# An S5 mixer's input projection taken four row groups at a time, in four PSUM banks, with the pieces around it in a new sequence

## The chip, the cores and the metric

The kernel runs on one core of a Trainium2 chip. TensorE (PE) multiplies matrices, VectorE (DVE) and ScalarE (ACT) do elementwise work, GpSimd (POOL) and SyncE (SP) mostly issue transfers, and here GpSimd does some additions too. Each engine works its own queue in order. The metric is device time in microseconds (us) of one execution, lower is better.

## The reference, cut to what matters

The program is two transformer blocks on 256 tokens of width 1024, all in fp32. The first block puts 16 meta tokens ahead, normalises, projects to 5640 columns and feeds two mixers from them. The S5 mixer, which the change touches, is a diagonal complex recurrence per group of 16 channels (32 groups, 64 states each):

```python
def _s5_mixer(u, lam_re, lam_im, log_dt, b_re, b_im, c_re, c_im, d_skip):
    uf = u.astype(f32).reshape(bsz, length, S5_GROUPS, S5_GROUP)
    ...
    bu = jnp.einsum("gph,blgh->blgp", b_bar, uf.astype(jnp.complex64))
    a = jnp.broadcast_to(lam_bar, (1, length, S5_GROUPS, S5_STATE))
    _, state = lax.associative_scan(_linear_recurrence_combine, (a, bu), axis=1)
    y = jnp.real(jnp.einsum("ghp,blgp->blgh", c_mat, state))
    return y + d_skip * uf

for layer in range(DEPTH):          # first block
    p = h @ w_in[layer] + b_in[layer]
    u_s5, q, k, v, o_pre, i_pre, f_pre, g_s5, g_m = _split_columns(p)
    y_s5 = _s5_mixer(u_s5, ...)
    z = jax.nn.gelu(y_s5) @ s5_w_glu[layer]
    y_s5 = z[..., :D_MODEL] * jax.nn.sigmoid(z[..., D_MODEL:])
    hm = _mlstm_mixer(q_h, k_h, v_h, i_pre, f_pre)
    y_m = (jax.nn.sigmoid(o_pre) * _head_norm(hm, ...)) @ m_w_out[layer]
    mix = jax.nn.sigmoid(g_s5) * y_s5 + jax.nn.sigmoid(g_m) * y_m
    h = _layer_norm(ALPHA * h + mix @ w_o[layer], ...)
    # then the FFN
```

The second block (block attention, gated delta rule, a mixture of experts) follows and is not touched.

## The kernel before, in words

**The projection and its fillers.** `block1` projects in pieces of 256 columns (`in_proj`). A piece is two halves of 24 matmuls each (`ps_mm<-hTh,whi`, `hTl,whi`, `hTh,wlo`: the fp32 product from rounded high and low parts); each half fills one of the two `ps_mm` banks, and ScalarE empties it (`gth`). The weights of a piece come as `w`; ScalarE rounds them to `whi`, VectorE takes `wlo = w - whi`, and for a share of the pieces a GpSimd transfer forms `wlo` (L614). After each piece of v, og, gs and gm (four each, in this order) the S5 mixer is advanced by some pieces of its own, the mLSTM mixer by some of its own. `SCHED` is the list of S5 pieces per projection piece; what is left after gm runs behind the last projection piece (`step(s5, 100)`).

**The S5 mixer.** It works on four blocks c of 128 channels (eight groups of channels on 128 partitions, in four row groups r of 32 partitions). Its pieces are:

- `meta`: the 16 meta tokens.
- `elem(c, rr)`: for each row group of `rr` one `ps_acc` bank, the input projection (`ps_acc<-u,BT`, 32 rows of the array), and `turn`, which rotates the phases: two VectorE operations that read the bank (`s5z<-ps_acc,rot` and `s5t<-ps_acc,rot`) and two GpSimd additions (`s5z<-s5z,s5t`). `s5t` has two buffers.
- `chain(c)`: the recurrence, four times a carry (`s5c`, small `s5z` operations) and two scans over 256 elements (L821).
- `prod(c, rr)`: the rotation back, `s5q<-s5z,rot` and `s5z<-s5z,rot`, one of each for each row group.
- `cproj(c)`, which follows `prod(c, (2, 3))` in its piece: the output projection (`ps_acc<-s5q,CT` and `ps_acc<-s5z,CT`, 32 columns of the array each), then the skip term and GELU on `u`: VectorE `u<-u,FA,ps_acc`, ScalarE `gel_t`, VectorE `gel_t` twice, ScalarE `gel_w`, VectorE `u<-gel_w,u`.

PSUM holds two `ps_mm` banks and six `ps_acc` banks. A scheduler puts each engine's instructions in an order at build time, from the dependences and its own costs; `SCHED` and the sequence of pieces shape it.

**The other mixer.** For each of four heads the mLSTM mixer forms `mw` and `mwm` (ScalarE, then VectorE from `ps_acc`), multiplies them with the values (`ps_acc<-vt,mw` and `ps_acc<-vt,mwm`, 12 matmul instructions that are called a vt group here) and takes statistics (`bn_s`). After the fourth head a chain of 8-column VectorE operations, here the **rsqrt chain** (`mve`, `rs_y`, `rs_t`, `mc`, `mnb`), gives the scale; ScalarE then scales all heads (`qk<-qk,mnb,mc` x8), PE transposes them (`ps_acc<-ident,qk`) and VectorE gates them (`og`).

**The mix.** After the projection, the output matrices of both mixers are streamed through the same weight buffers; the first matmuls there are `ps_mm<-ymh,whi`.

Of the kernel before, what the change touches and what calls it, by code (L numbers as in the profile page):

```python
# [83 lines left out]
PP = [9]  # L84
L1A = [2, 2, 2, 2]
ORD = "abcdefmnopyz"
SCHED = [2, 2, 2, 2, 2, 2, 1, 1, 1, 1, 1, 1, 1, 1]


def dap(t, offset, *dims):  # L90
# [3 lines left out]
class K:  # L94
# [660 lines left out]
    def s5(self, pool):  # L755
# [3 lines left out]
        def bcast(v, *lead):  # L759
            shp = [128] + list(lead) + list(v.shape[1:])  # L760
            for _ in lead:
                v = v[:, None]
            return v.to_broadcast(shp)
# [3 lines left out]
        def turn(dst, src, cos, sin, tmp, eng):  # L767
            self.tt(dst, src, cos, OP.mult)
            self.tt(tmp, src, sin, OP.mult)
            self.tt(dst[:, 0], dst[:, 0], tmp[:, 1], OP.add, eng=eng)  # L770
            self.tt(dst[:, 1], dst[:, 1], tmp[:, 0], OP.subtract, eng=eng)
# [19 lines left out]
        def elem(c, rr):  # L791
            ps = {}
            if c not in Z:
                Z[c] = pool.tile([128, 4, 2, 4, 64], F32, name="s5z", bufs=2)
            for r in rr:
                ps[r] = self.ps("acc")
            for i in range(2):
                for r in rr:
                    rs = slice(32 * r, 32 * r + 32)
                    self.mm(ps[r][:, 256 * i:256 * i + 256], self.BT[i][rs, c, :], self.u[rs, c, 16:], True, True)  # L800
            for r in rr:
                z = Z[c][:, :, :, r, :].rearrange("p j i t -> p i j t")
                p = ps[r].rearrange("p (i j t) -> p i j t", i=2, j=4)
                t = pool.tile([128, 2, 4, 64], F32, name="s5t", tag="s5t", bufs=2)
                turn(z, p, *[bcast(self.rot[i][:, 4 * c + r], 2, 4) for i in range(2)], t, G)

        def chain(c):
            gs = slice(4 * c, 4 * c + 4)
            d = flat(self.decay[:, gs])
            last = tail[c]  # L810
            for j in range(4):
                z = Z[c][:, j]
                first = z[:, :, :, 0]
                t = pool.tile([128, 2, 2, 4], F32, name="s5c", bufs=2)
                for i in range(2):
                    self.tt(t[:, i], last, self.carry[:, j > 0, i, None, gs].to_broadcast([128, 2, 4]), OP.mult)
                self.tt(first, first, t[:, 0], OP.add)
                self.tt(first[:, 0], first[:, 0], t[:, 1, 1], OP.subtract)
                self.tt(first[:, 1], first[:, 1], t[:, 1, 0], OP.add)
                for i in range(2):  # L820
                    self.V.tensor_tensor_scan(flat(z[:, i]), d, flat(z[:, i]), 0.0, OP.mult, OP.add)  # L821
                last = z[:, :, :, 63]

        def prod(c, rr):
            if c not in Q:
                Q[c] = pool.tile([128, 4, 2, 4, 64], F32, name="s5q")
            for r in rr:
                z, q = (v[:, :, :, r, :].rearrange("p j i t -> p i j t") for v in (Z[c], Q[c]))
                for i, o in ((0, q), (1, z)):
                    self.tt(o, z, bcast(self.rot[i][:, 4 * c + r], 2, 4), OP.mult, eng=G if r in PP and i == 0 else None)  # L830

        def cproj(c):
            p = self.ps("acc")
            for n, (ct, i, z) in enumerate(((0, 0, 0), (1, 1, 1), (2, 0, 1), (2, 1, 0))):
                for r in range(4):
                    rs = slice(32 * r, 32 * r + 32)
                    self.mm(p[rs, :256], self.CT[ct][:, c, rs], (Q, Z)[i][c][:, :, z, r, :], n == 0, n == 3)
            ur = self.u[:, c, 16:]
            self.stt(ur, ur, self.FA[:, 92 + c:93 + c], p[:, :256], OP.mult, OP.add)
            if "ys5" in self.dbg:  # L840
                self.nc.gpsimd.dma_start(self.dbg["ys5"][c * 128:(c + 1) * 128, :], ur)
            t = self.cv.tile([128, 256], F32, name="gel_t", tag="cv_y", bufs=2)
            w = self.cv.tile([128, 256], F32, name="gel_w", tag="cv_t", bufs=2)
            self.act(t, ur, AF.Square)
            self.ts(t, t, 0.044715, OP.mult, 1.0, OP.add)
            self.tt(t, t, ur, OP.mult)
            self.act(w, t, AF.Tanh, scale=math.sqrt(2.0 / PI))
            self.stt(ur, w, 1.0, ur, OP.add, OP.mult)
# [1 line left out]
        meta()  # L850
        yield
        for c in range(5):
            if c < 4:
                elem(c, (0, 1))
                yield
            if c:
                prod(c - 1, (0, 1))
                yield
            if c < 4:
                elem(c, (2, 3))  # L860
                yield
            if c:
                prod(c - 1, (2, 3))
                cproj(c - 1)
                yield
            if c < 4:
                chain(c)
                yield
# [151 lines left out]
    def block1(self):  # L1020
# [38 lines left out]
        s5 = self.s5(work)  # L1059
        n5 = iter(list(SCHED) + [0] * 30)  # L1060
        mo = self.mlstm_out()
# [5 lines left out]
        for i in range(4):  # L1067
            self.in_proj(1536 + 256 * i, 0, lambda c0, j, p: self.evac_v(work, c0 - 12 + j, p),
                         lambda: step(s5, next(n5)))
        for i in range(4):  # L1070
            self.in_proj(2560 + 256 * i, 16, lambda c0, j, p: self.evac_gate(
                work, self.og, 2 * i + j, 0, p, self.halfg[:, 2 * i + j:2 * i + j + 1]),
                lambda: (step(ml, 2), step(s5, next(n5))))
        step(ml, 10)
        for k, dst in ((0, self.gs), (1, self.gm)):
            for i in range(4):
                self.in_proj(3592 + 1024 * k + 256 * i, 16, lambda c0, j, p: self.evac_gate(
                    work, dst, 2 * i + j, 8 + 8 * k, p, self.hc[:, k:k + 1]),
                    lambda: (step(mo, 1), step(s5, next(n5))))
# [1109 lines left out]
```

## Time and profile before

| | |
|---|---|
| time, three runs | 939.01, 930.54, 942.08 us (median 939.01) |
| profiled execution, device time | 939.74 us |
| its span, first to last instruction | 938.0 us |
| mean granted TensorE clock | 0.961 |
| PE busy | 885.8 us, 94% of the span |
| DVE, ACT, POOL busy | 572.8, 429.4, 62.9 us |
| stretch with the mixers | about 95 to 248 us |

The span is what the profiler sees between the first and the last instruction; the device time holds 1.7 us more. Busy shares are averages over the program: in the mixer stretch VectorE and GpSimd have a larger part of the work than afterwards. A granted clock of 1.00 is 2.4 GHz, 0.50 is 1.2 GHz.

### The profile page before, as it was taken

To read this page: it belongs to the slowest core of one execution; us is meant where nothing else is said; L and a number is where in the kernel's file an instruction comes from. 1 tells how busy PE (TensorE), PEld (TensorE's weight loads), DVE (VectorE), ACT (ScalarE), POOL (GpSimd) and SP (SyncE) were. 2 spreads that over 40 slices of the span, in tenths; PEclk is the share of its full clock that TensorE was granted. 3 is DMA by queue.
4 is the path that set the end of the run, shared out by engine and by line. 5 is a ranking of instruction groups with operands and counts; after the bars stand their busy time and mean duration, and the time that the engine had idled before them with its cause. 6 is when DMAs were issued, how large, how long until landed. Compare 5 with 4: busy or idle time off the path is not lost.

```text
span 938.0 us, 16064 instructions
## 1 busy us (share of the span) xinstructions
PE 885.8 (94%) x6204; PEld 670.7 (72%) x6204; DVE 572.8 (61%) x1457; ACT 429.4 (46%) x828; POOL 62.9 (7%) x91
## 2 busy tenths in 40 slices
PE   7998989998999999999998999999989999999993
PEld 6997857688999899998887998886654443444431
DVE  6688797757689667665578798666463222323213
ACT  4485444485766146564452366577442111222102
POOL 2012332122000000000000010000000000000000
PEclk7899897899999999999999999999999999999997
DMA  7887654478696356656773543334969999999971
GB/s 187 193 201 174 159 116 101 100 159 202 205 296 216 115 180 180 181 180 194 258 263 95 180 134 99 129 121 163 398 240 342 377 400 408 409 408 403 405 254 49
DMA packets 134708, 208.05 MB, mean 222 GB/s; under 512 B 13801, under 2 KB 99026, under 8 KB 134626
## 3 DMA queue, kind: packets, MB, share of 16 engines
q1 hardware_dynamic: 131458, 195.95, 62.4%
q0 software_dynamic: 2880, 10.49, 6.0%
q8 instruction: 51, 0.84, 0.4%
q10 hardware_dynamic: 288, 0.52, 0.2%
q14 instruction: 31, 0.25, 0.1%
HBM read 195.40 MB, written 1.05 MB: 209 GB/s over the span
## 4 chain that ended last, share of the span: by engine, by line
PE 74%; DVE 12%; ACT 6%; DMA 5%; issue 2%; POOL 0%; SPq 0%; ACTq 0%; POOLq 0%; DVEq 0%
PE ps_acc L133 43%; PE ps_mm L133 25%; PE ps_wo L133 3%; PE ps_acc L137 2%; DVE wlo L140 2%; DVE s5z L821 2%; ACT whi L155 2%; DMA wlo<-w 1%; DMA w<-in_w_in_dram 1%; DVE cv_y L149 1%; ACT mo_P L152 1%; DVE s5z L140 1%; DMA w<-in_w_up_dram 1%; DMA w<-in_m_w_out_dram 1%; DMA ln_g<-in_ln_g_dram 1%
## 5 line engine op out<-in xcount | busy, mean ns | idle before, releaser
L155 ACT ACTIVATE whi<-w 128x1024 fp32r<-128x1024 f32 x150 | 157.8, 1056 | 149.7 <-PE ps_mm L133 90.0
L140 DVE TENSOR_TENSOR wlo<-w,whi 128x1024 fp32r<-128x1024 f32 x130 | 160.0, 1232 | 85.2 <-ACT whi L155 84.6
L133 PE MATMUL ps_mm<-hph,whi 128*128 128x256 f32 x424 | 122.1, 288 | 0.0
L133 PE MATMUL ps_mm<-hph,wlo 128*128 128x256 f32 x424 | 120.8, 285 | 0.0
L133 PE MATMUL ps_mm<-hpl,whi 128*128 128x256 f32 x424 | 120.4, 284 | 0.0
L133 PE MATMUL ps_acc<-w,xg 128*64 128x512 f32 x512 | 117.8, 599 | 0.0
L133 PE MATMUL ps_mm<-hTh,whi 128*128 128x256 f32 (+1 forms) x360 | 108.2, 301 | 4.1 <-ACT gth L152 2.8
L133 PE MATMUL ps_mm<-hTh,wlo 128*128 128x256 f32 (+1 forms) x360 | 105.9, 294 | 2.7 <-DVE wlo L140 2.0
L133 PE MATMUL ps_mm<-hTl,whi 128*128 128x256 f32 (+1 forms) x360 | 105.8, 294 | 0.0
L133 PEld LDWEIGHTS ps_acc<-w,xg 128*64 128x64 f32 x512 | 35.6, 137 | 68.2 <-issue 64.1
L133 PEld LDWEIGHTS ps_mm<-hph,whi 128*128 128x128 f32 x424 | 79.9, 189 | 1.8 <-issue 1.8
L133 PEld LDWEIGHTS ps_mm<-hph,wlo 128*128 128x128 f32 x424 | 79.9, 188 | 1.2 <-issue 1.2
L133 PEld LDWEIGHTS ps_mm<-hpl,whi 128*128 128x128 f32 x424 | 79.9, 188 | 0.6 <-issue 0.6
L133 PEld LDWEIGHTS ps_mm<-hTh,whi 128*128 128x128 f32 x360 | 71.4, 199 | 9.5 <-ACT gth L152 3.1
L133 PEld LDWEIGHTS ps_mm<-hTh,wlo 128*128 128x128 f32 x360 | 71.3, 198 | 3.5 <-DVE wlo L140 2.2
L133 PEld LDWEIGHTS ps_mm<-hTl,whi 128*128 128x128 f32 x360 | 71.4, 198 | 1.2 <-issue 1.2
L152 ACT ACTIVATE mth<-ps_acc,cb 128x256 f32<-128x256 f32 x16 | 7.6, 475 | 119.8 <-PE ps_acc L133 119.8
L133 PE MATMUL ps_acc<-w,mhT 128*32 128x512 f32 x512 | 61.3, 594 | 1.0 <-DVE mhT L2011 1.0
L149 DVE SCALAR_TENSOR_TENSOR mth<-mth,ps_acc 128x256 f32<-128x256 f32 x16 | 6.7, 421 | 82.5 <-ACT mth L152 82.5
L140 DVE TENSOR_TENSOR hpl<-ps_acc,hph 128x512 fp32r<-128x512 f32 x40 | 26.1, 687 | 50.6 <-ACT hph L155 50.6
L155 ACT ACTIVATE hph<-ps_acc 128x512 fp32r<-128x512 f32 (+1 forms) x44 | 23.8, 576 | 64.0 <-PE ps_acc L133 61.5
L133 PEld LDWEIGHTS ps_acc<-w,mhT 128*32 128x32 f32 x512 | 20.1, 110 | 35.6 <-issue 30.5
(603 smaller groups left out, 1772.5 us busy)
## 6 DMA issues: line engine op xcount, KB each, us to landing
w<-in_w_down_dram SPq DMA_DIRECT2D x46, 1024.0 KB, 13.6
w<-in_w_gate_dram SPq DMA_DIRECT2D x60, 512.0 KB, 10.4
w<-in_w_up_dram SPq DMA_DIRECT2D x60, 512.0 KB, 7.2
w<-in_w_in_dram SPq DMA_DIRECT2D x41, 512.0 KB, 4.4
w<-in_w_in_dram SPq DMA_DIRECT2D x16, 1024.0 KB, 8.9
w<-in_w_up_dram SPq DMA_DIRECT2D x16, 1024.0 KB, 5.7
wlo<-w POOLq DMA_DIRECT2D x20, 512.0 KB, 5.1
w<-in_m_w_out_dram SPq DMA_DIRECT2D x4, 1024.0 KB
```

The source lines that it names most:

```text
L133: self.PE.matmul(out, lhsT, rhs, start=start, stop=stop, **kw)
L137: self.PE.transpose(out, in_, self.ident[:n, :n])
L140: (eng or self.V).tensor_tensor(out, a, b, op)
L149: (eng or self.V).scalar_tensor_tensor(out, a, s, b, op0, op1, **kw)
L152: self.S.activation(out, in_, func, bias=bias, scale=scale, **kw)
L155: self.S.activation(out, in_, AF.Copy)
L821: self.V.tensor_tensor_scan(flat(z[:, i]), d, flat(z[:, i]), 0.0, OP.mult, OP.add)
```

## The change

`elem` is called once for each block with all four row groups, so that its 16 matmul instructions write four `ps_acc` banks, and not twice with two. The piece that held its second half is gone, and the sequence for a block c is now: the first two products of block c-1, `elem(c)`, the other two products and the output projection of c-1, the chain of c. That makes 17 pieces of 21, and `SCHED` places them anew: 20 of its pieces ran inside the projection and one behind it before; now all 17 run by the last piece of gs, none in gm.

```diff
-SCHED = [2, 2, 2, 2, 2, 2, 1, 1, 1, 1, 1, 1, 1, 1]
+SCHED = [2, 2, 1, 2, 1, 2, 1, 2, 1, 1, 1, 1]
...
         for c in range(5):
-            if c < 4:
-                elem(c, (0, 1))
-                yield
             if c:
                 prod(c - 1, (0, 1))
                 yield
             if c < 4:
-                elem(c, (2, 3))
+                elem(c, (0, 1, 2, 3))
                 yield
             if c:
                 prod(c - 1, (2, 3))
                 cproj(c - 1)
                 yield
             if c < 4:
                 chain(c)
                 yield
```

| projection piece | S5 pieces before | S5 pieces after |
|---|---|---|
| v0 to v3 | meta, e0a; e0b, ch0; e1a, p0a; e1b, p0b | meta, e0; ch0, p0a; e1; p0b, ch1 |
| og0 to og3 | ch1, e2a; p1a, e2b; p1b; ch2 | p1a; e2, p1b; ch2; p2a, e3 |
| gs0 to gs3 | e3a; p2a; e3b; p2b | p2b; ch3; p3a; p3b |
| gm0 to gm3 | ch3; p3a; none; none | none |
| behind the projection | p3b | none |

(e is `elem`, ch `chain`, p `prod`; a is row groups 0 and 1, b is 2 and 3; `cproj(c)` is part of p b.)

The instructions are the same on every engine; their order differs from the first S5 piece to the start of the mix, and the SyncE queue is unchanged.

VectorE, between the chain and the products of block 0. Before:

```order
L140 TENSOR_TENSOR s5z_1458<-ps_acc_1459,rot0_556 128x2x4x64
L140 TENSOR_TENSOR s5t_1465<-ps_acc_1459,rot1_557 128x512
L140 TENSOR_TENSOR s5z_1458<-ps_acc_1460,rot0_556 128x2x4x64
L140 TENSOR_TENSOR s5t_1470<-ps_acc_1460,rot1_557 128x512
L140 TENSOR_TENSOR s5q_1475<-s5z_1237,rot0_556 128x2x4x64 x2
L140 TENSOR_TENSOR s5z_1237<-s5z_1237,rot1_557 128x2x4x64 x2
L140 TENSOR_TENSOR s5q_1475<-s5z_1237,rot0_556 128x2x4x64 x2
L140 TENSOR_TENSOR s5z_1237<-s5z_1237,rot1_557 128x2x4x64 x2
L140 TENSOR_TENSOR wlo_1765<-w_1761,whi_1764 128x1024
L140 TENSOR_TENSOR s5z_1458<-ps_acc_1558,rot0_556 128x2x4x64
```

After, from the second row of the products (`s5z_1237` is block 0 in both, its products are the rows that read it with `rot`; rows that read a `ps_acc` are the turns of block 1):

```order
L140 TENSOR_TENSOR s5z_1237<-s5z_1237,rot1_557 128x2x4x64 x2
L140 TENSOR_TENSOR s5q_1380<-s5z_1237,rot0_556 128x2x4x64
L140 TENSOR_TENSOR s5z_1463<-ps_acc_1464,rot0_556 128x2x4x64
L140 TENSOR_TENSOR s5t_1476<-ps_acc_1464,rot1_557 128x512
L140 TENSOR_TENSOR s5z_1463<-ps_acc_1465,rot0_556 128x2x4x64
L140 TENSOR_TENSOR s5t_1481<-ps_acc_1465,rot1_557 128x512
L140 TENSOR_TENSOR s5z_1463<-ps_acc_1466,rot0_556 128x2x4x64
L140 TENSOR_TENSOR s5t_1486<-ps_acc_1466,rot1_557 128x512
L140 TENSOR_TENSOR s5z_1463<-ps_acc_1467,rot0_556 128x2x4x64
L140 TENSOR_TENSOR s5t_1491<-ps_acc_1467,rot1_557 128x512
L140 TENSOR_TENSOR s5z_1237<-s5z_1237,rot1_557 128x2x4x64
L140 TENSOR_TENSOR s5q_1380<-s5z_1237,rot0_556 128x2x4x64
```

All four turns of block 1 now stand between the third and the last products of block 0; before, two stood ahead of all products and two behind them.

VectorE, at the rsqrt chain after the fourth head. Before:

```order
L149 SCALAR_TENSOR_TENSOR rs_y_2174<-rs_t_2175,rs_y_2174 128x8
L140 TENSOR_TENSOR rs_t_2175<-rs_y_2174 128x8
L149 SCALAR_TENSOR_TENSOR rs_t_2175<-rs_t_2175,mve_2168 128x8
L149 SCALAR_TENSOR_TENSOR rs_y_2174<-rs_t_2175,rs_y_2174 128x8
L140 TENSOR_TENSOR mc_2167<-mc_2167,rs_y_2174 128x8
L149 SCALAR_TENSOR_TENSOR mnb_2187<-mc_2167,mst_1671 128x8
L140 TENSOR_TENSOR s5z_2269<-ps_acc_2270,rot0_556 128x2x4x64
```

After, from the last turn of block 3 on (`s5z_2172` is block 3):

```order
L140 TENSOR_TENSOR s5z_2172<-ps_acc_2176,rot0_556 128x2x4x64
L140 TENSOR_TENSOR s5t_2200<-ps_acc_2176,rot1_557 128x512
L140 TENSOR_TENSOR rs_t_2213<-rs_y_2212 128x8
L140 TENSOR_TENSOR wlo_2444<-w_2440,whi_2443 128x1024
L149 SCALAR_TENSOR_TENSOR rs_t_2213<-rs_t_2213,mve_2206 128x8
L140 TENSOR_TENSOR s5z_2172<-s5z_2172,s5c_2408 128x8
L149 SCALAR_TENSOR_TENSOR rs_y_2212<-rs_t_2213,rs_y_2212 128x8
L140 TENSOR_TENSOR s5z_2172<-s5z_2172,s5c_2408 128x4 x2
L140 TENSOR_TENSOR rs_t_2213<-rs_y_2212 128x8
L821 SCALAR_TENSOR_TENSOR s5z_2172<-s5decay_558,s5z_2172 128x256
L149 SCALAR_TENSOR_TENSOR rs_t_2213<-rs_t_2213,mve_2206 128x8
L821 SCALAR_TENSOR_TENSOR s5z_2172<-s5decay_558,s5z_2172 128x256
```

The four turns of block 3 now stand inside the rsqrt chain, of which the excerpt has the last, and behind them a weight's `wlo`, the first carries and two scans of `chain(3)`; `mnb` follows five rows further down.

ScalarE, at the scaling of the heads. Before:

```order
L155 ACTIVATE whi<-w 128x1024
L152 ACTIVATE gth<-ps_mm,bh 128x256
L152 ACTIVATE wlo<-w 128x1024
L152 ACTIVATE qk<-qk,mnb,mc 128x256 x8
L152 ACTIVATE gs<-gth,hc 128x256
L152 ACTIVATE gth<-ps_mm,bh 128x256
L155 ACTIVATE whi<-w 128x1024
```

After (`gel_t` and `gel_w` belong to the GELU of block 2):

```order
L155 ACTIVATE whi<-w 128x1024
L152 ACTIVATE qk<-qk,mnb,mc 128x256 x8
L152 ACTIVATE gel_t<-u 128x256
L155 ACTIVATE whi<-w 128x1024
L152 ACTIVATE wlo<-w 128x1024
L152 ACTIVATE gel_w<-gel_t 128x256
L152 ACTIVATE gth<-ps_mm,bh 128x256
```

The next `gth` now stands behind the scaling and the GELU of block 2, with two weights' rounding between them.

## Rows read from the trace of the kernel before

**Rows 1.** From the page: busy time of the engines, and PE's busy tenths and granted clock in 40 equal slices of the span (23.45 us each).

```profile
PE 885.8 (94%) x6204; PEld 670.7 (72%) x6204; DVE 572.8 (61%) x1457; ACT 429.4 (46%) x828; POOL 62.9 (7%) x91
...
PEclk7899897899999999999999999999999999999997
```

**Rows 2.** Busy time of each engine in four stretches of the mixers (us busy, number of instructions, then granted clock, DMA share, GB/s).

```profile
119.20:130.00 10.80, 8.82 (x62) 5.13 (x61) 10.80 (x16) 2.25 (x5) 5.64 (x7) 0.84 0.66 147
130.00:153.00 23.00, 20.53 (x105) 15.85 (x103) 19.29 (x52) 10.20 (x22) 6.80 (x8) 0.78 0.48 115
153.00:182.00 29.00, 27.14 (x166) 18.82 (x166) 20.11 (x57) 12.95 (x31) 5.54 (x6) 0.88 0.49 110
...
222.60:248.00 25.40, 22.22 (x188) 20.61 (x187) 14.44 (x24) 18.07 (x30) 1.73 (x2) 0.93 0.83 225
```

**Rows 3.** PE's waits between 95 and 275 us: what waited for what, us in total, times, longest.

```profile
PE ps_acc L133 <- DVE mwm L149: 4.3, 2, 2.5
PE ps_mm L133 <- ACT gth L152: 2.8, 1, 2.8
PE ps_acc L133 <- DVE s5q L140: 2.0, 2, 1.7
PE ps_mm L133 <- DVE gm L140: 1.1, 1, 1.1
```

**Rows 4.** PE's timeline at two of the input projections (start, duration of the group, number of records; the next row's start ends it), and at one vt group with its successor.

```profile
95.06 2.08 PE L133 MATMUL ps_acc<-u,BT 32*128 32x256 f32 x8
...
104.04 1.13 PE L133 MATMUL ps_acc<-u,BT 32*128 32x256 f32 x8
105.11 0.39 PE L133 MATMUL ps_mm<-hTh,whi 128*128 128x272 f32 x1
...
159.46 1.13 PE L133 MATMUL ps_acc<-vt,mw 128*128 128x257 f32 x4
160.53 0.70 PE L133 MATMUL ps_acc<-u,BT 32*128 32x256 f32 x4
```

**Rows 5.** PE's timeline at the output projection of block 0 and the projection matmul behind it (in brackets the idle time before the row and who ended it).

```profile
121.45 0.62 PE L133 MATMUL ps_acc<-s5q,CT 128*32 128x256 f32 x2
...
124.66 1.24 PE L133 MATMUL ps_acc<-s5q,CT 128*32 128x256 f32 x3 [1.72 <-DVE s5q L140]
...
128.55 0.39 PE L133 MATMUL ps_mm<-hTh,whi 128*128 128x256 f32 x1
```

**Rows 6.** VectorE's timeline from the chain of block 0 to the products of block 0.

```profile
110.44 0.45 DVE L140 TENSOR_TENSOR s5z<-s5z,s5c 128x8 f32<-128x8 f32 x3 [1.32 <-POOL s5z L140]
...
117.82 0.67 DVE L140 TENSOR_TENSOR s5z<-ps_acc,rot 128x512 f32<-128x512 f32 x1
118.40 0.68 DVE L140 TENSOR_TENSOR s5t<-ps_acc,rot 128x512 f32<-128x512 f32 x1
...
120.19 2.08 DVE L140 TENSOR_TENSOR s5q<-s5z,rot 128x512 f32<-128x512 f32 x2
...
125.13 1.28 DVE L140 TENSOR_TENSOR s5z<-s5z,rot 128x512 f32<-128x512 f32 x2
126.33 1.21 DVE L140 TENSOR_TENSOR wlo<-w,whi 128x1024 fp32r<-128x1024 f32 x1
```

**Rows 7.** GpSimd's timeline: the additions of two row groups (four instructions), once beside turns and once beside products.

```profile
100.38 2.84 POOL L140 TENSOR_TENSOR s5z<-s5z,s5t 128x256 f32<-128x256 f32 x4 [13.55 <-DVE s5t L140]
...
119.17 3.68 POOL L140 TENSOR_TENSOR s5z<-s5z,s5t 128x256 f32<-128x256 f32 x4 [5.37 <-DVE s5t L140]
```

**Rows 8.** Windows of 2 us, as in rows 2: behind the stop at 124.66, and around a short stop before 266.

```profile
125.00:127.00 2.00, 2.00 (x17) 0.81 (x18) 2.00 (x4) 0.00 (x0) 0.00 (x0) 0.50 0.87 164
...
264.00:266.00 2.00, 1.19 (x11) 0.98 (x9) 1.46 (x2) 1.46 (x2) 0.00 (x0) 1.00 1.07 364
266.00:268.00 2.00, 1.75 (x15) 1.78 (x16) 1.79 (x3) 1.65 (x2) 0.00 (x0) 1.00 0.83 266
```

**Rows 9.** PE's timeline at the first, third and fourth vt group (the fourth's last row).

```profile
140.15 0.70 PE L133 MATMUL ps_acc<-vt,mwm 16*128 16x257 f32 x2 [2.47 <-DVE mwm L149]
...
171.31 0.70 PE L133 MATMUL ps_acc<-vt,mwm 16*128 16x257 f32 x2 [1.86 <-DVE mwm L149]
...
190.41 1.13 PE L133 MATMUL ps_acc<-vt,mw 128*128 128x257 f32 x4
```

**Rows 10.** The rsqrt chain and what hangs on it: VectorE's first and last row of it, ScalarE's scaling, PE's first transposition.

```profile
191.66 0.42 DVE L338 BATCH_NORM_STATS2 bn_s<-ps_acc 128x6 f32<-128x256 f32 x1
...
195.58 0.17 DVE L149 SCALAR_TENSOR_TENSOR mnb<-mc,mst 128x8 f32<-128x8 f32 x1
...
196.22 4.03 ACT L152 ACTIVATE qk<-qk,mnb,mc 128x256 f32<-128x256 f32 x8
...
196.86 0.33 PE L137 MATMUL ps_acc<-ident,qk 128*128 128x128 f32 x1
```

**Rows 11.** ScalarE at the GELU of block 2 and PE's next projection matmul.

```profile
221.58 0.42 ACT L152 ACTIVATE gel_t<-u 128x256 f32<-128x256 f32 x1 [3.92 <-DVE u L149]
224.08 0.42 ACT L152 ACTIVATE gel_w<-gel_t 128x256 f32<-128x256 f32 x1 [2.09 <-DVE gel_t L140]
...
225.86 0.39 PE L133 MATMUL ps_mm<-hTh,whi 128*128 128x256 f32 x1 [2.83 <-ACT gth L152]
```

**Rows 12.** PE at the end of the projection: the output projection of block 3 and the first matmul of the mix.

```profile
245.21 0.64 PE L133 MATMUL ps_acc<-s5q,CT 128*32 128x256 f32 x8
...
247.48 0.50 PE L133 MATMUL ps_mm<-ymh,whi 128*128 128x256 f32 x2 [0.34 <-ACT ymh L155]
```

## Prediction, on record before the result

> **What bounds the kernel now.** I read the page's busy times and its 40 slices first. PE is busy for 94% of the span [rows 1], so a change can win only what PE stands still, what it does at half clock, or work that it is spared; whatever it wins in the first block, the later stages carry to the end, since they are untouched and PE-bound too. The slices show a granted clock of 1.0 nearly everywhere but in the first quarter. So the next view is the stretches of the mixers: there PE has 0.78 to 0.93 of full clock, and in each of these stretches it is idle for some us [rows 2]. The waits name the causes [rows 3]: PE stands for `mwm`, for `gth`, for `s5q`, some 9 us in all. The half clock comes behind these stops: 0.50 in the 2 us behind the stop of 1.72 [rows 5, 8]. Its price is the stretch times what the clock lacks: 10.8 x 0.16 = 1.7, 23 x 0.22 = 5.1, 29 x 0.12 = 3.5 and 25.4 x 0.07 = 1.8 us [rows 2], 12.1 together, 3.0 for a stop on average. A stop of 0.81 us ahead of 266 has clock 1.00 on both sides [rows 8]. So what the kernel can gain here is about 9 + 12 us, and the question is not whether VectorE has time on average but at which moments PE arrives before it.
>
> **The input projection itself.** One piece of two row groups takes 1.06 us at full clock (104.04 to 105.11) and 2.0 at half clock [rows 4]. Its eight instructions last as long as four full-height ones of the vt group (1.07 us, 159.46 to 160.53) [rows 4], so two row groups do run side by side. No row shows four of them side by side. Bounds: 1.06 for all 16 instructions if they do (4.2 us of PE saved over the program), 2.12 if they don't (nothing saved). I take 1.06, since two groups lost nothing. For four row tiles the Trainium skill (TensorE: Matmul & The Clock Gate, Part 3: Packing small matmuls, measured speedup) gives 3.07x, not 4x; by that 16 instructions of 0.27 us would take an estimated 1.4 us, and the sum below would come out 0.7 us higher. The two side by side here (2.0x) neither bear that out nor contradict it.
>
> **Block 0: earlier start, longer stop.** At the start all four turns of block 0 follow each other. GpSimd needs 1.42 us for a row group beside turns (2.84 for two) [rows 7]; from 100.38 four of them end at about 106, and the chain starts there and not at 110.44, where it had waited 1.32 for GpSimd [rows 6]. From 106 VectorE has, in its new order: the chain 7.4 (110.44 to 117.82), a `wlo` 1.2, five products at 0.6, all eight turn operations of block 1 at 0.6 (117.82, 118.40) [rows 6]: about 122.4. Then the last products, with GpSimd's additions beside them: two took 2.08 there rather than 1.2 [rows 6]. The first of them end at 124.4, the last, behind another `wlo`, at 126.8. PE is there earlier, since two input projections before it are spared: 121.45 - 2.1 = 119.3 [rows 5]. It works off the last group at half clock in 2 us and leaves the output projection at about 129.0, 0.45 later than now (128.55). As the stop is some 7 us rather than 2, I add 0.75 of half clock: **1.2 us lost.** The four spared projections of this part are worth nothing, they become waiting. By the Trainium skill (SBUF — State Buffer, Who interferes with whom) a VectorE operation with two SBUF inputs and a GpSimd operation that reads SBUF exclude each other, and one that reads PSUM does not; the 3.68 us of additions beside products against 2.84 beside turns [rows 7] agree. Eight turns in a row are by that the good place for the additions, which is in the sum.
>
> **Heads one to four.** PE came to the first vt group at 137.68 and stood 2.47 [rows 9]. After, it comes 1.2 later and behind four more projection matmuls (0.12 each): 139.4. VectorE, from 126.8: chain 7.4, a `wlo` 1.2, the GELU's four operations 1.6, three products 1.8, `mw` and `mwm` 0.9, together 139.7. So the stop shrinks to 0.3, and the 5.1 us of half clock behind it go. The stop of 1.86 at the third group with its 3.5 goes likewise [rows 2, 9]. New ones come: a `ps_mm` bank waits for a `gth` that now stands behind block 0's or 1's `gel_w` (rows 11 show what such a place costs: up to 2.8), worked out at 1.2; and `mwm` of the third head stands behind turns, worked out at 1.05 (between 0 and the 2.5 of rows 9). Both are too short, I take it, to bring the half clock. With one input projection spared (1.06): -1.2 - 0.3 + 2.47 + 5.1 + 1.86 + 3.5 + 1.06 - 1.2 - 1.05 = **10.2 ahead** at the fourth vt group; with that of block 3, 11.3.
>
> **The rsqrt chain.** Here it is given back. Now `mnb` is done 4.2 us after the fourth vt group (191.55 to 195.75), ScalarE scales the heads (4.03 for eight) and PE's first transposition runs at 196.86 [rows 10], with no stop over 0.3. After, the eight turn operations of block 3 stand inside that chain (4.8 us), a `wlo` (1.2), a wait for GpSimd and the carries (1.0) and two scans (1.3): 4.2 + 8.3 = 12.5 us after the vt group, and the first scaled head at 13.0. PE has the input projection (1.06), 66 projection matmuls (7.9) and small gaps until it needs it: 9.4. It stops for 3.5 us, and the half clock follows. The next obstacle is close: the output projection of block 3 has one matmul in PE's queue ahead of the next projection piece, and its `s5q` stands on VectorE behind the rest of the chain (some 9 us behind `mnb`), 21.3 after the vt group. The `gth` for the next bank, behind the scaling, GELU and two weight roundings on ScalarE, comes at about the same time. PE without stops would be at 13.4. Loss 7.9, whichever part of it is stop and which half clock: 11.3 - 7.9 = **3.4 ahead.** Bounds: 3.5 (one stop and no half clock) to 11 (both stops and twice 3.0).
>
> **The last pieces and the mix.** The stop of 2.83 behind block 2's GELU [rows 11] goes with its 1.8 of half clock: that GELU is over by then, and block 3's stands with its VectorE steps next to each other. 8.0 ahead. The output projection of block 3 leaves the end of the projection (245.21 to 247.0) [rows 12]; in return nothing is won, since the weights of the mix come on a chain that starts from the last projection pieces and ends at the short stop before 266 [rows 8]: that stop grows from 0.8 to 2.5. 6.3 ahead at 266. All stops of 1.72 and longer in these rows were followed by half clock, so I take the cheapest of the four, 1.8, for this one: **4.5 ahead.** The weight transfers that GpSimd issues come behind up to eight additions rather than four; four additions take 2.8 to 3.7 us [rows 7], so a transfer that had no slack would cost PE that much; I take 0, since no row of PE's waits names such a transfer [rows 3].
>
> **Sum.** 939.74 - 4.5 = 935.2. The profiled execution lies 0.7 over the median of the runs (939.01), so 935 stands for both.
>
> **Rivals.**
> (1) *Slower: short stops also bring the half clock.* The forecast has stops of about 1.0 to 1.4 us at the `gth` of block 0's GELU, at the third `mwm` and at `s5q` of block 3 without one. No row has a stop between 0.81 (not followed) and 1.72 (followed) [rows 5, 8]. If the line lies at 1 us, three more half clocks of 3.0 make 944, slower than before. It decides from a stop of about 1 us.
> (2) *The rsqrt chain is not late.* If PE comes to the transposition later, or VectorE gets through the turns sooner (GpSimd's part in it is an estimate), the stop of 3.5 falls under 1 us and its half clock goes: 6 to 7 us better, 928. For it: the sum for VectorE is 12.5 with nothing overlapped. Against it: the order is fixed and all of its parts have rows.
> (3) *The pieces don't do what they say:* four row groups in four banks take 2.12 us. Block 2 and 3 then lose 1.06 each, block 0 starts its turns later by 2 at half clock and passes that on to the first stop, about half of it: 938. By the rows that two groups share the array at no loss I hold this unlikely.
>
> **How the numbers follow.** Forecast 0.45 (931 to 938), slower 0.25, rival 2 0.2, rival 3 0.1. The range reaches from 926, rival 2 with the mix's half clock gone too, to 944, rival 1. 2% are 18.8 us, about what a measurement of this kernel can tell from no change (its three runs lie 11.5 us apart); all stops, half clocks and spared projections together are some 25 us, so over 2% faster takes nearly all of them: 0.04. Over 2% slower needs new stops at more places than the order shows: 0.04. Within 2%: 0.92.
>
> **What the profile after would show.** PE's `u,BT` in four groups of 16 records, 1.1 us each at full clock (2.1: rival 3). A stop of 6 to 8 us for `s5q` or `s5z` at 119 to 127, and none over 0.5 at the first vt group. Clock 1.00 from about 132 to 165. A wait for ScalarE's `qk` at about 190 of 3 to 4 us, with the clock at 0.50 behind it, and one for `s5q` or `gth` at about 200. No stop over 1 us in the pieces of gm. I would be wrong if the clock falls around 160 to 170 (rival 1) or if PE is not stopped at `ident,qk` (rival 2).

## The result, and the profile after

The changed kernel takes 942.37 us (median of 20 runs, 937.40 to 945.97); the kernel before, beside it, 937.48 (20 runs). The ratio is 1.0052 (95% interval 1.0033 to 1.0072): **slower by half a percent**, less than the 2% of the verdict, but the interval lies above 1. The forecast was 935, faster by half a percent. A later measurement gave 942.11 (12 runs) and 1.0057 (1.0028 to 1.0087).

The profiled execution says the opposite: 937.79 us, 2 us less than that of before. So the profile alone can't explain the result, and one of the questions below is why. First what it shows, against [rows 1 to 3]: busy times, four of the stretches (and 182 to 205, which had no stop over 0.3 us before), and PE's waits in the mixers.

```profile
PE 877.2 (94%) x6204; PEld 664.6 (71%) x6204; DVE 573.4 (61%) x1457; ACT 430.2 (46%) x828; POOL 61.0 (7%) x91
...
PEclk7898989989999999999999999998999999999997
```

```profile
119.20:130.00 10.80, 5.95 (x41) 3.43 (x42) 9.26 (x23) 0.65 (x2) 4.63 (x6) 0.68 0.66 153
130.00:153.00 23.00, 22.91 (x156) 17.34 (x158) 15.87 (x43) 14.10 (x33) 1.72 (x2) 1.00 0.55 127
153.00:182.00 29.00, 27.20 (x187) 21.06 (x176) 25.78 (x73) 14.99 (x35) 8.36 (x10) 0.94 0.48 110
182.00:205.00 23.00, 16.50 (x127) 12.94 (x126) 22.35 (x60) 14.32 (x24) 8.27 (x10) 0.90 0.57 131
...
222.60:248.00 25.40, 22.92 (x188) 22.03 (x187) 10.36 (x20) 18.60 (x37) 1.72 (x2) 1.00 0.93 244
```

```profile
PE ps_acc L133 <- DVE s5q L140: 6.8, 2, 4.7
PE ps_acc L137 <- ACT qk L152: 4.5, 1, 4.5
PE ps_mm L133 <- ACT gth L152: 1.8, 1, 1.8
PE ps_mm L133 <- ACT ymh L155: 1.6, 1, 1.6
PE ps_acc L133 <- DVE s5z L140: 1.6, 1, 1.6
PE ps_mm L133 <- DMA wlo<-w: 0.6, 1, 0.6
```

The half clock between 130 and 153 and the waits for `mwm` are gone; instead PE is idle for 6.5 us between 182 and 205. The stops one by one, from PE's timeline, with the two ends of the rsqrt chain on VectorE (answering to [rows 4, 5, 9, 10]):

```profile
92.88 2.09 PE L133 MATMUL ps_acc<-u,BT 32*128 32x256 f32 x16
...
108.94 1.15 PE L133 MATMUL ps_acc<-u,BT 32*128 32x256 f32 x16
110.01 0.39 PE L133 MATMUL ps_mm<-hTh,whi 128*128 128x272 f32 x1
...
122.49 0.63 PE L133 MATMUL ps_acc<-s5q,CT 128*32 128x256 f32 x1 [4.73 <-DVE s5q L140]
125.13 0.61 PE L133 MATMUL ps_acc<-s5z,CT 128*32 128x256 f32 x1 [1.56 <-DVE s5z L140]
...
161.95 0.39 PE L133 MATMUL ps_mm<-hTh,whi 128*128 128x256 f32 x1 [1.80 <-ACT gth L152]
...
179.96 0.43 DVE L338 BATCH_NORM_STATS2 bn_s<-ps_acc 128x6 f32<-128x256 f32 x1 [0.84 <-PE ps_acc L133]
...
192.60 0.17 DVE L149 SCALAR_TENSOR_TENSOR mnb<-mc,mst 128x8 f32<-128x8 f32 x1
...
193.46 0.47 PE L137 MATMUL ps_acc<-ident,qk 128*128 128x128 f32 x1 [4.48 <-ACT qk L152]
202.23 0.59 PE L133 MATMUL ps_acc<-s5q,CT 128*32 128x256 f32 x2 [2.02 <-DVE s5q L140]
...
244.13 0.51 PE L133 MATMUL ps_mm<-ymh,whi 128*128 128x256 f32 x2 [1.57 <-ACT ymh L155]
```

### The profile page after: what moved, and what is told of

Same layout as the page of the kernel before. It is cut to its first block, busy times and chain, and to the rows that moved or that the text cites. A ratio compares the mean times of both kernels' runs of the same rounds, so it can differ in the third digit from the quotient of the medians.

```text
span 936.0 us, 16073 instructions
## 1 busy us (share of the span) xinstructions
PE 877.2 (94%) x6204; PEld 664.6 (71%) x6204; DVE 573.4 (61%) x1457; ACT 430.2 (46%) x828; POOL 61.0 (7%) x91
## 3 DMA queue, kind: packets, MB, share of 16 engines
HBM read 195.40 MB, written 1.05 MB: 210 GB/s over the span
## 4 chain that ended last, share of the span: by engine, by line
PE 70%; DVE 9%; ACT 5%; issue 1%; DMA 1%; POOL 1%; ACTq 0%; POOLq 0%; DVEq 0%
PE ps_acc L133 41%; PE ps_mm L133 24%; PE ps_wo L133 4%; PE ps_acc L137 2%; DVE wlo L140 2%; ACT whi L155 1%; DMA wlo<-w 1%; DVE cv_y L149 1%; ACT mo_P L152 1%; DVE s5z L821 1%; POOL s5z L140 1%; ACT h L155 1%; DVE r L149 0%; ACT g_FW L155 0%; DVE s5z L140 0%
## 5 line engine op out<-in xcount | busy, mean ns | idle before, releaser
L133 PEld LDWEIGHTS ps_acc<-w,xg 128*64 128x64 f32 x512 | 35.4, 137 | 67.8 <-issue 64.5
L133 PEld LDWEIGHTS ps_acc<-w,mhT 128*32 128x32 f32 x512 | 20.2, 110 | 35.6 <-issue 30.4
```

The source lines that it names most:

```text
L133: self.PE.matmul(out, lhsT, rhs, start=start, stop=stop, **kw)
```

## The experiments

Each execution lists its time and its mean granted clock. Time x (1 - clock) is what half clock took from PE in it, time x clock is the rest (full-clock work and idle time). This table has the averages over the timed runs and is used throughout. The mean clock is listed to three decimals, so the split of a single execution is good to half a us. Each kernel was compared with runs of the kernel before on the same chip; these are four sets in all, the clocks are from three of them. The sets are: changed; merge_only and rsqrt_first; changed again, late_block3 and merge_products_first; the other four. Between sets the ratios to before are the safer comparison, and the text gives both where they differ.

| kernel | runs | median us | ratio to before (95%) | half clock us | rest us |
|---|---|---|---|---|---|
| before (four sets) | 107 | 937.5, 939.4, 939.0, 938.1 | | 33.6 to 34.5 | 903.5 to 904.0 |
| changed | 20 | 942.4 | 1.0052 (1.0033 to 1.0072) | 35.2 | 906.7 |
| changed, again | 12 | 942.1 | 1.0057 (1.0028 to 1.0087) | 35.6 | 906.5 |
| merge_only | 12 | 936.1 | 0.9968 (0.9942 to 0.9994) | 34.0 | 901.3 |
| rsqrt_first | 12 | 940.1 | 1.0020 (0.9997 to 1.0044) | 33.8 | 905.7 |
| late_block3 | 12 | 933.9 | 0.9976 (0.9948 to 1.0003) | 33.7 | 900.2 |
| merge_products_first | 12 | 933.2 | 0.9959 (0.9927 to 0.9991) | 33.7 | 899.6 |
| sequence_only | 12 | 943.4 | 1.0062 (1.0032 to 1.0091) | 36.2 | 907.0 |
| bank_turned | 12 | 938.7 | 1.0020 (0.9993 to 1.0047) | 32.2 | 905.6 |
| merge_best | 12 | 932.1 | 0.9952 (0.9921 to 0.9983) | 32.5 | 899.6 |
| late_best | 12 | 930.7 | 0.9940 (0.9908 to 0.9971) | 30.2 | 900.4 |

**Both kernels again.** No edit.

> The kernel before once more, for a second profiled execution. Theory M (the change of the time is made in the mixers, between the first input projection of S5 and the first matmul of the FFN): that stretch took 218.8 us in the first profile (95.06 to 313.90); here it takes 214 to 217, since the first profile lies 2.3 us over the median. Theory O (the change is made outside, by where the half clock falls at the start and in the block attention): the stretch stays within 1 us of 218.8 and the rest moves.

> The kernel before, a third profiled execution. Theory M (the half clock behind one and the same stop differs from execution to execution): the stops of the mixers at the same places and lengths within 0.3 us, the half clock behind at least one of them of another length than in the first two. Rival (the half clock is fixed by the stop): the same stretches again, 3.4, 10.2, 6.8 and 3.4 us.

> The changed kernel once more, for a second profiled execution; its first one (937.8) is the second fastest of its 20 runs. Theory M: the mixer stretch, 216.6 us in the first profile (92.88 to 309.44), takes 219 to 224 here, with more half clock behind the stops at gth (1.8 us at 162), qk (4.5), s5q (2.1) and ymh (1.6). Theory O: the stretch stays within 1 us of 216.6 and the half clock behind the stop for mo_P near 640 or at the start makes the rest longer.

> The changed kernel once more, timed beside the others. Split of an execution's time into what the half clock takes (time x (1 - mean clock)) and the rest: in the first 20 runs of the change 35.2 and 906.7 us, in 23 of before 34.5 and 904.0. Theory M (more idle time in the mixers, 17 us for 10, less 4.2 us of spared projections, and the half clock not less than before over many executions): the rest again 2 to 3.5 us over before's, the half clock within 1.5 of it, 0.3 to 0.6% slower. Rival (the first measurement was of its chip): within 0.2% of before.

The profiled executions of before took 939.74, 939.62 and 941.20 us, those of the changed kernel 937.79, 939.71 and 936.96. The stretch from the first input projection to the FFN took 218.8, 219.3 and 219.2 before and 216.6, 217.1 and 216.2 after: theory M's stretches (214 to 217 before, 219 to 224 after) were not seen, and both stayed within 1 us of the first profiles, as theory O has it. The timed runs of the changed kernel came out as theory M of the last expectation has them: the rest 3.0 us over before's, half clock 1.2 over, 0.57% slower. All profiled executions of the changed kernel lie under its medians by 2.4 to 5.4 us, those of before over theirs by 0.2 to 2.3. By the split, profiled executions of before lose 36.6 to 38.5 us to half clock (timed 33.6 to 34.5), those of the change 30.0 to 34.8 (timed 35.2, 35.6), while the rest differs by 2.4 us in the profiled and by 2.5 to 3.2 in the timed ones. So it is the half clock on which profile and timing disagree, far more than the rest. Why the profiled executions fall where they do is open; three executions of each kernel are few, since half clock alone differs by 8 to 13 us between the timed executions of one kernel.

In the three profiles of before the half clock in the mixers stands in the same stretches, so the rival held there. For the changed kernel it did not. Here is PE in two of its executions, windows of 2 us at and behind the stop of 1.80 for `gth` (idle in the first row of each; PE's busy time comes first, the clock third from the right); first the first profile, then the third:

```profile
160.00:162.00 2.00, 0.20 (x2) 0.05 (x1) 1.42 (x6) 0.88 (x3) 0.55 (x1) 1.00 0.00 0
162.00:164.00 2.00, 2.00 (x12) 2.00 (x13) 1.97 (x9) 1.83 (x6) 0.00 (x0) 0.69 0.00 0
164.00:166.00 2.00, 2.00 (x12) 2.00 (x11) 1.93 (x8) 1.72 (x5) 0.00 (x0) 0.50 0.00 0
```

```profile
159.00:161.00 2.00, 0.20 (x2) 0.08 (x1) 1.45 (x6) 0.91 (x3) 0.52 (x1) 1.00 0.00 0
161.00:163.00 2.00, 2.00 (x17) 2.00 (x18) 1.97 (x9) 1.82 (x6) 0.00 (x0) 1.00 0.00 0
```

The same stop in the same kernel is followed by half clock once and not the other time. In the second profile it is followed by half clock too, so twice of three times.

**The merge without the new sequence.** Against the kernel before:

```diff
-                elem(c, (0, 1))
+                elem(c, (0, 1, 2, 3))
                 yield
...
             if c < 4:
-                elem(c, (2, 3))
                 yield
```

> The input projection of all four row groups in one piece, at the place of the first half of before, with the numbers and the sequence of before for all else (an empty piece where the second half was). Theory M with the sequence as cause: no turns inside the rsqrt chain beyond those of before's place for block 3, no stop at ident,qk over 1 us; 3 us faster to 2 slower than before. Rival (merging itself is the cause: all turns and additions of a block together hold VectorE up ahead of the products of the block before): a stop of 5 to 7 us at the output projection of block 0, and 3 to 6 us slower than before.

It is faster than before by 3 us, so the four banks are a gain. Theory M holds, at the edge of its range, and the rival is right about one thing: the stop at the output projection of block 0 is there (4.7 and 1.3 us), and yet the kernel is faster. The stop at `ident,qk` is 0.6 us.

**The sequence without the merge.** Against the changed kernel, `elem(c, (0, 1, 2, 3))` becomes `elem(c, (0, 1))` and `elem(c, (2, 3))` in one piece.

> The new sequence and numbers of pieces, but each input projection in two halves of two row groups and two banks, both in one piece. Theory M (the sequence is the loss, the merge a gain of 2 to 4 us of spared projections): the turns of block 3 stand inside or ahead of the rsqrt chain here too, the stop at ident,qk is 3 us or more; 0 to 5 us slower than the changed kernel, 5 to 10 slower than before. Rival (the four banks together are what hurts): faster than the changed kernel by 2 us or more.

943.4 us, 5.3 over before and 1 over the change; PE stops 5.6 us at `ident,qk`. The loss in the mixers is in the sequence, not in the banks' number. The 1 us hides what the merge is worth here: sequence_only is free of a later stop that the changed kernel has (its own section below). bank_turned is the changed kernel without that stop, on the same chip, and takes 938.7, so the merge gives back 4.7 us by the medians.

**The rsqrt chain.** Against the changed kernel, from `c = pool.tile(...)` to the scaling in `mlstm`:

```diff
+        with self.tc.high_priority(offset=200):
```

> The changed kernel with the rsqrt chain of the mLSTM mixer at a higher priority, so that its rows alternate with the turns of block 3 and stand ahead of the wlo, the carries and the scans. Theory M (the stop at ident,qk and what follows costs 5 to 8 us): the stop of 4.5 us shrinks under 1, the half clock behind it goes, the s5q stop moves; 3 to 7 us faster than the changed kernel, so 2 us faster to 2 slower than before. Rival (VectorE is simply too late as a whole there, so that the stop only moves to s5q of block 3): less than 2 us faster than the changed kernel.

By the medians 2.0 to 2.3 us faster than the change, under the 3 to 7 of the first theory; by the ratios to before 3.0 to 3.5, its low end. The runs don't decide between it and the rival's "less than 2". Its rows now alternate with the turns of block 3, so `mnb` ends 8.2 us behind the fourth vt group's statistics and not 12.8, and the stop is 2.4 rather than 4.5. It did not fall under 1. The `s5q` stop became one of 1.77 for a `gth`, and behind it came one of 2.26 for a weight's transfer at 213 us.

**Block 3 one piece later.** Against the changed kernel:

```diff
-SCHED = [2, 2, 1, 2, 1, 2, 1, 2, 1, 1, 1, 1]
+SCHED = [2, 2, 1, 2, 1, 2, 1, 1, 1, 1, 1, 1, 1]
```

> The changed kernel with block 3 one projection piece later (the list is 2, 2, 1, 2, 1, 2, 1, 1, 1, 1, 1, 1, 1), so that its turns stand behind the whole rsqrt chain on VectorE; blocks 0 to 2 are as in the change. Theory M (the stops at ident,qk and s5q of block 3, 4.5 and 2.0 us, are the loss): both go, idle time in the mixers 6 us less, 4 to 7 us faster than the changed kernel, under before by 0 to 3. Rival (the late VectorE work only moves on: the chain and output projection of block 3 then collide with the gates and the start of the mix): a new stop of 2 us or more between 200 and 245, and less than 2 us faster than the changed kernel.

8 us faster than the change, measured beside it: 6.3 of the rest and 1.9 of half clock by the averages. Under before it is 5 us by the medians and 0.24% by the ratio, whose interval reaches 1.0003. Now the turns of block 3 stand behind `mnb`, which is done 6.2 us behind the statistics, and the two stops (4.5 and 2.0) are two of 0.6:

```profile
180.01 0.43 DVE L338 BATCH_NORM_STATS2 bn_s<-ps_acc 128x6 f32<-128x256 f32 x1 [0.84 <-PE ps_acc L133]
...
185.99 0.17 DVE L149 SCALAR_TENSOR_TENSOR mnb<-mc,mst 128x8 f32<-128x8 f32 x1
...
186.84 0.33 PE L137 MATMUL ps_acc<-ident,qk 128*128 128x128 f32 x1 [0.61 <-ACT qk L152]
...
188.80 0.33 PE L137 MATMUL ps_acc<-ident,qk 128*128 128x128 f32 x1 [0.58 <-ACT qk L152]
```

No new stop over 1.6 us followed. So the one number of the list that puts block 3's input projection ahead of the rsqrt chain carries the loss in the mixers. The edit moves the S5 pieces behind that projection one projection piece later too; rsqrt_first, which moves the rsqrt chain and the scaling alone, gets back 2 to 3.5 of the 8 us.

**Products ahead of turns.** Against merge_only, `with self.tc.high_priority(offset=100):` around the loop of `prod`; on VectorE three products of block 0 pass the eight turn operations of block 1, elsewhere nothing moves.

> As merge_only, but the products have a higher priority; on PE, ScalarE and GpSimd nothing moves, on VectorE only the last products of block 0 go ahead of the turns of block 1. Theory M (the stop at block 0's output projection is eight turn operations of 0.6 us standing ahead): the 4.7 and 1.3 us there become 1 to 2 us together, the half clock behind it shorter; 3 to 5 us faster than merge_only, 5 to 8 faster than before. Rival (the chain of block 1 then starts later and the first vt group waits instead): the stop there grows from 0.5 to 3 us or more and the time is within 2 us of merge_only.

2.9 us faster than merge_only by the medians, just under the theory's 3 to 5, and 0.8 by the ratios, whose intervals overlap; so a gain over merge_only is not shown. The rival is partly right: the stop at the first vt group grew, from 0.47 to 1.70, though not to 3. The 4.7 and 1.3 became 1.26, but PE then stood 3.39 for a `gth` behind the GELU of block 0, which came earlier with the output projection:

```profile
119.58 0.64 PE L133 MATMUL ps_acc<-s5q,CT 128*32 128x256 f32 x8 [1.26 <-DVE s5t L140]
131.52 0.58 PE L133 MATMUL ps_mm<-hTh,whi 128*128 128x256 f32 x1 [3.39 <-ACT gth L152]
```

**A stop 390 us further on.** The rows of the queues are the same from the mix on, but the waits are not. `set_psum(acc=4, wo=4)` gives the output product of the second block banks that were `ps_acc` banks until then. Which bank held which tile depends on the order in which the six banks were taken since the start, and the mixers of the change take them in another order. Before, bank 0, which the first `ps_wo` tile gets, had held an earlier `ps_acc` tile; the first tile runs without a wait, and only the second waits, in bank 3, for the last `ps_acc` tile but one. After, bank 0 had held the last `ps_acc` tile, which ScalarE reads last (`mo_P`), and the first tile waits for it. The rows there, ScalarE's first `mo_P` of this step and then PE's: before, changed, and with the rotation turned by one:

```profile
638.79 0.37 ACT L152 ACTIVATE mo_P<-ps_acc,mo_s 128x128 f32<-128x128 f32 x1 [2.24 <-DVE mo_s L1575]
...
640.62 0.47 PE L133 MATMUL ps_wo<-whi,mx2h 128*128 128x512 f32 x1
...
643.01 0.50 PE L133 MATMUL ps_wo<-whi,mx2h 128*128 128x512 f32 x1 [1.46 <-ACT mo_P L152]
...
648.18 0.43 PE L133 MATMUL ps_acc<-mo_PT,mvt 128*64 128x128 f32 x2 [0.21 <-ACT mo_PT L158]
```

```profile
633.31 0.37 ACT L152 ACTIVATE mo_P<-ps_acc,mo_s 128x128 f32<-128x128 f32 x1 [2.23 <-DVE mo_s L1572]
...
637.97 0.80 PE L133 MATMUL ps_wo<-whi,mx2h 128*128 128x512 f32 x1 [2.61 <-ACT mo_P L152]
...
646.19 0.43 PE L133 MATMUL ps_acc<-mo_PT,mvt 128*64 128x128 f32 x2
```

```profile
638.12 0.37 ACT L152 ACTIVATE mo_P<-ps_acc,mo_s 128x128 f32<-128x128 f32 x1 [2.23 <-DVE mo_s L1573]
...
639.92 0.47 PE L133 MATMUL ps_wo<-whi,mx2h 128*128 128x512 f32 x1
...
642.78 0.70 PE L133 MATMUL ps_acc<-mqk 64*128 64x256 f32 x4 [1.22 <-ACT mo_P L152]
...
647.49 0.43 PE L133 MATMUL ps_acc<-mo_PT,mvt 128*64 128x128 f32 x2 [0.21 <-ACT mo_PT L158]
```

From the first to the last row shown the step takes 9.4, 12.9 and 9.4 us. The other two profiles of the changed kernel have 11.8 and 11.7, with less half clock behind the stop. The window behind the stop in the changed kernel, and one of the same length in the kernel before:

```profile
640.00:644.00 4.00, 4.00 (x19) 1.82 (x18) 1.63 (x5) 2.20 (x6) 0.00 (x0) 0.50 0.00 0
```

```profile
644.00:648.00 4.00, 3.97 (x28) 2.49 (x28) 3.37 (x8) 4.00 (x12) 0.00 (x0) 1.00 0.00 0
```

The fourteen profiles of this document divide cleanly here. Seven have the stop of 2.6 us, half clock behind it, and a step of 11.5 to 13.0 us: the three of the changed kernel, merge_only, rsqrt_first, late_block3 and merge_products_first. Seven have a stop of 1.2 to 1.5 us, clock 1.00 and a step of 9.4 us: the three of before, sequence_only, bank_turned, merge_best and late_best. So it is the four banks taken at once that bring bank 0 to the last tile, and not the sequence; and the stop costs 2.2 to 3.6 us in the profiles. The edit of the third, against the changed kernel:

```diff
         self.mix(poolC)
+        for _ in range(1): self.V.memset(self.ps("acc")[:1, :1], 0.0)
         pC.close()
```

> The changed kernel, and after the mix one element of one more ps_acc bank is set to zero, so that the rotation of the six ps_acc banks is one further from there on (nothing else moves). In the stage with the block attention and the gated delta rule, the first ps_wo tile of the output product takes bank 0, and in the changed kernel bank 0 is that of the last ps_acc tile before it, which ScalarE reads last (mo_P); PE stands 2.6 us there, 1.5 before. Theory B (the change has shifted that rotation, and part of its loss arises there, 390 us behind the mixers): the stop for mo_P falls under 1 us, that stage takes 49 to 51 us between the same two matmuls where all changed kernels took 52 to 54, and the kernel is 2 to 4 us faster than the changed one. Rival (all of the loss is in the mixers): the time stays within 1.5 us of the changed kernel's 942.

938.7, that is 3.4 to 3.7 us under the changed kernel by the medians and 3.0 to 3.5 by the ratios, whose intervals (1.0033 to 1.0072 and 1.0028 to 1.0087 against 0.9993 to 1.0047) overlap. The averages put 1.0 of it in the rest (906.6 to 905.6) and 3.2 in half clock (35.4 to 32.2). Theory B holds in the time; its stop is gone from `ps_wo`, but one of 1.22 us for `mo_P` is left further on, not under 1.

**The best of both.** merge_products_first and, for late_best, late_block3 with products ahead of the turns, both with the rotation turned.

> merge_products_first (one piece for four row groups, the sequence and numbers of before, products ahead of the turns) with the rotation of the banks one further after the mix. Theory B: 2 to 4 us faster than merge_products_first (933.2), so 929 to 932, 0.7 to 1.0% under before. Rival: within 1.5 us of 933.

> late_block3 with products ahead of the turns and the rotation of the banks one further after the mix. Theory M with B: 2 us for the products (the stop of 4.7 and 1.6 at block 0's output projection becomes shorter) and 2 to 4 for the banks: 928 to 931 where late_block3 had 933.9. Rival: within 1.5 us of late_block3.

932.1 and 930.7. late_best is the fastest, 0.6% under before (ratio 0.9940, 0.9908 to 0.9971) and 11 us under the change; the two fixes are worth 3.2 us on late_block3, the turned banks 1.1 on merge_products_first (0.7 by the ratios). The last is less than theory B's 2 to 4, and there the rival's range holds, although the step is 9.4 us in the profile of merge_best and 11.7 in that of merge_products_first. The intervals of these two steps overlap with no gain, so the price of the far stop is between about 1 and 3.7 us and not known better.

## Why the prediction was wrong, step by step

**The mechanism in the mixers was right in its places.** Four row groups run side by side: 16 instructions in 1.07 us (108.94 to 110.01), as long as eight took before, and as taken. Sixteen times 0.27 us in 1.07 is 4.0x. The Trainium skill (TensorE: Matmul & The Clock Gate, Part 3: Packing small matmuls) has 3.07x for four row tiles (of 512 columns, here 256), by which sixteen would take an estimated 1.4 us; the measured 1.07 differs from it and decides. Nearly every place named came: the `s5q` and `s5z` stop of block 0 (forecast some 7 us, measured 4.73 + 1.56), none at the first vt group, `gth` (1.2; 1.80), `ident,qk` (3.5; 4.48, since the first transposition ran 13.6 us behind the vt group and not 13.0, and PE was there after 9.1 and not 9.4), `s5q` of block 3 (1.0 to 1.4; 2.02), the start of the mix (2.5 before 266; 1.57 + 0.33 at its start instead). The third `mwm` stop (1.05) came once in three profiles. The rest of the sum, without half clock, was put at about +0.3 us; over timed runs without the far stop it is +2.0 (905.6 against 903.6), and three stops came out longer by 0.6 to 1.0 us. The stretch from the first input projection to the FFN is 2.5 us shorter in the profiles on average, where the forecast had 4.5.

**A term put at nothing: the weight transfers of GpSimd.** The forecast took 0 for them, since no row of before waits for one. In the three profiles of the changed kernel PE waits 0.57, 1.57 and 1.30 us for `DMA wlo<-w` in the pieces of gm, where no stop over 1 us was forecast; in those of before it doesn't.

**Mis-sized: the half clock.** The forecast's gain of 4.5 us was 4.8 less half clock (10.4 that goes: 5.1, 3.5 and 1.8; about 5.7 that comes: 0.75, some 3.1 of the 7.9, and 1.8) and 0.3 more of the rest. Against the profile the half clock was nearly right: behind the stops of the mixers half clock takes 11.9 us before and 8.5 after, 3.4 less. Over timed executions half clock takes 33.6 to 34.5 us before and 35.2 to 35.6 after; without the far stop 32.2, 1.4 to 2.3 less. I priced it from one execution, with stops as its cause and a length as its condition, and the same stop of 1.80 is followed by half clock in one execution and not in the next. The runs of before list clocks of 0.957 to 0.971, some 13 us of spread; the term had to be carried with that uncertainty, and the rest alone, +0.3 with its bounds, was no reason for "faster".

**Failed: "whatever it wins in the first block, the later stages carry to the end, since they are untouched".** They are untouched in their rows and not in their banks. That was no term, no bound and no rival, and it cost 3.4 to 3.7 us by the medians, 2.2 to 3.6 in the profiles (on merge_products_first only 1.1 by the medians). Without it the kernel is at 938.7, just over the forecast's 931 to 938, and no longer shown to differ from before (ratio 1.0020, 0.9993 to 1.0047): most of the loss goes, but the gain that was forecast does not come. Taken apart by the medians of one chip, the new sequence costs 5.3 us (sequence_only) and the merge gives 4.7 back (bank_turned); the banks cost their part on top of that.

**The rivals.** The first (slower, 944) has nearly the right time, in part by luck. Its sign, a clock that falls around 160 to 170, came in two of three profiles, but behind a stop of 1.80 us and not of 1 to 1.4, and most of the loss is idle time in the sequence plus the far stop. Its bounds were misread too: the stop ahead of 266 that the forecast has as 0.81 us is 1.06 long, of which the window up to 266 shows 0.81 ([rows 3], the wait for `gm`), and clock 1.00 stands behind it; in the second profile of before it is 1.6 long, with clock 1.00 behind it as well. The second (rsqrt chain not late) is what late_block3 made true: 8 us, forecast 6 to 7. The third fell by the 16 records in 1.07 us.

## What to carry to other kernels

Split every run into time x (1 - clock) and time x clock, and forecast them apart: the second comes from stops, most of which the forecast above had to within 1 us, the first is an average over executions, not a row of one profile. When a change takes buffers in another order, look at where a rotating pool changes hands, however far on: compare the waits of both programs there, not only the order of their rows. A short chain of tiny operations that a late engine waits for is the wrong place to put long work in front of, and moving one entry of a list by one place was worth more than the merge.

## What the runs showed of the hardware

Stops of about the same length leave half clock behind in one execution and none in another: in rsqrt_first stops of 1.77 to 2.40 us at 164, 190, 200 and 211 were followed by clock 1.00 throughout, in the changed kernel 1.80 and 2.02 were followed by 0.50 twice of three times. Rows of the stops of 2.40 and of the 4 us behind it:

```profile
192.47 0.33 PE L137 MATMUL ps_acc<-ident,qk 128*128 128x128 f32 x1 [2.40 <-ACT qk L152]
```

```profile
189.00:193.00 4.00, 1.60 (x19) 1.19 (x21) 3.91 (x9) 1.70 (x5) 3.97 (x5) 1.00 0.25 61
193.00:197.00 4.00, 4.00 (x46) 2.61 (x39) 2.67 (x11) 3.35 (x7) 1.20 (x2) 1.00 0.00 0
```

At another place the division was clean: behind the far stop of 2.6 us half clock stood in all seven profiles that have it, and where it is 1.2 to 1.5 us the clock stayed at 1.00 in all seven. What sets the one place apart from the other is open.

And whole executions of one kernel on one chip differ by 12 us (before: 929.7 to 941.9 in 35 runs), most of it in the mean clock: half clock takes 27.0 to 38.6 us of them, the rest is 900.9 to 906.0.
